# One hybrid attention and scan step on one core: the first projections with features outside, attention with one set of scores

## The chip, the cores and the metric

The kernel runs on one core of one Trainium2 chip. A core has TensorE (PE, matrix products; the loading of stationary operands is shown apart as PEld), VectorE (DVE), ScalarE (ACT), GpSimd (POOL) and SyncE (SP), each with its own row of instructions that it works off in order. PE writes into PSUM, which has eight banks of 512 columns of fp32 in 128 partitions; the other engines read them there. The metric is the device time of one execution in microseconds (us). PE's clock has two levels, 2.4 and 1.2 GHz; "granted clock" is the mean over a stretch in shares of the upper one.

## The reference, cut to what matters

One step of a network with two layers for 128 context tokens and 512 latent tokens of width 1024. The even layer's mixer is attention (8 heads of 64, 2 heads of keys and values, so four query heads share one) beside a gated delta rule (4 heads, both directions); the odd layer's mixer is a state-space scan; each layer also has an MLP. The change touches the first norm, the attention part of the first projection, and attention:

```python
h = _modulate(x, norm_mix_g[layer], sh1, sc1)     # rms norm over features, * (1 + scale) + shift
aq, ak, av, dqkv, dz, dbeta, dalpha = _split(h @ w_in, EVEN_SPLITS)
...
def attend(q_blk):
    s = jnp.einsum('bqhgd,bkhd->bhgqk', q_blk, k, preferred_element_type=F32) * scale
    p = jax.nn.softmax(s, axis=-1).astype(v.dtype)
    return jnp.einsum('bhgqk,bkhd->bqhgd', p, v)
```

Context queries read the 128 context keys; latent queries read 512 latent keys and 256 keys of a cache. Shift and scale come from a vector of conditions by a product with `w_mod`, whose first 2048 columns this stage needs.

## The kernel before, in words

Data is fp32. A large product is split: operands become a high part in fp32r (`hh`, `whi`) and the rest (`hl`, `wlo`), and three fp32r products (`hh·whi`, `hh·wlo`, `hl·whi`) are summed in PSUM. A weight block arrives as `wraw` from HBM, ACT casts it to `whi`, DVE or GpSimd subtracts to `wlo` (`wpart`, L267 to L276; with `share` on, every other subtraction is GpSimd's). Products of attention's scores use fp32r with the high and low parts of queries and keys stacked in the 128 rows of the contraction; weights by values, sums and transposes ("turns", products with the unit matrix `ident`, named `con` in the trace) are in fp32. Which instruction stands where in an engine's row is set by a scheduler that plays the program through with estimated times when it is built; buffers ("pools" with a number of tiles) limit it.

*The start (0 to 88 us).* x, feature-major as `xt` (L727), is loaded in one transfer on ACT's queue. On SP's queue go eight blocks of modulation weights (1.05 MB each, `mod_first`, L497 to L522), and after the first two the weights of attention's first block. `token_r` (L568) works out the norms of one half of the tokens at a time: squares on ACT, sums by PE (`stps`, `stc`), an inverse square root by DVE, and a spreading by PE (`rbps`), copied to `rb`. `modulate` (L599) makes `htmp`, `hh` and `hl` for one feature tile and half after the other. The first projections (`atps`, L750) come in three blocks: 272 columns (gates, keys, values) and twice 256 (queries); for each block and each of five token tiles all eight feature tiles are summed, 24 products, into one of four PSUM tiles.

*Delta projections (88 to 225 us).* `delta_in` (`gps`, L300) projects for the four delta heads, with the preparation of keys (`att_prep`) beside it.

*Attention and delta heads (225 to 508 us).* `attention` is a generator that yields after each step; L775 sets the order in which the program is written, delta head 0, then nine times ten steps of attention, then delta heads 1 to 3; the scheduler mixes their instructions. Attention goes pair by pair of heads (four pairs). `front` makes the scores of a pair with the queries in the rows, only for their maxima (L1273; L1280 and L1285 on DVE). The negated maxima `nm` are turned (L1297) and written into extra rows of `qm`, which face rows of ones in `kst[1]`. `back` makes the scores again with the keys in the rows (L1303, L1304), now with the maximum taken off by those rows, ACT takes the exp (L1330) into a ring `pp` that lies in the raw weights' buffers, and PE multiplies by the values (L1331), where a column of ones gives the sums beside 64 columns of one head: for each pair 12 products of 512 columns. Sums are picked out (L1339), inverted (L1341), spread (L1347) and multiplied (L1350). Front of the next pair runs beside back of this one. Scores, turns and spreads share two PSUM tiles (`psc`), the products with values have one (`pat`).

*Then* the output projection (`by_rows`, `rps` L328) with weights through the same raw buffers, the MLP, the scan layer and its MLP.

## Time and profile before

| | us |
|---|---|
| median of 3 runs | 2151.09 (2150.94 to 2152.92) |
| the profiled execution's own time | 2148.23 |
| its span, first to last instruction | 2146.4 |
| PE busy | 2054.9 |
| DVE busy | 1373.3 |
| ACT busy | 898.4 |
| mean granted clock | 0.976 |

Busy times are those of single engines and overlap. The span is cut into 48 us of start, 40 us of first projections, 137 us of delta projections, 283 us of attention and delta heads up to the first product of the output projection at 512, and 1634 us of the rest. The time of the profiled execution is 2.9 us below the median of the timed runs.

### The profile page before, as it was taken

Reading aid. Unit: us, or ns where it says so; the run is one execution under the profiler, and the core shown is the slowest. Engines: PE = TensorE matmul, PEld = TensorE weight load, DVE = VectorE, ACT = ScalarE, POOL = GpSimd, SP = SyncE. Lnnn points to the kernel's source line nnn. Section 1 sums busy time; section 2 is a strip of 40 time slices with the busy share of each in tenths; the row PEclk is TensorE's granted clock in tenths of the full one; section 3 lists DMA queues with packets and bytes.
Section 4 is the critical chain, followed back from the end, with each engine's and each line's share of the span. In section 5 each row is a group of like instructions: output and inputs, shape, how many; then the busy total and the mean of one; then the engine's idle time right before and its main releaser. Section 6 shows DMA issues by size and latency. Waiting matters only on the chain.

```text
span 2146.4 us, 32954 instructions
## 1 busy us (share of the span) xinstructions
PE 2054.9 (96%) x13339; PEld 1846.3 (86%) x13339; DVE 1373.3 (64%) x2585; ACT 898.4 (42%) x1892; POOL 153.4 (7%) x112
## 2 busy tenths in 40 slices
PE   6999799899899999999899999999999899999998
PEld 4999787787797989898799999999888898989896
DVE  6376776865787767673678886787644734344445
ACT  4345444444342323233258876666531322323131
POOL 1041301300000000000000001111110000000000
PEclk9999799899999999999999999999999999999999
DMA  8261100005255344332224433343341221212121
GB/s 328 91 234 40 39 1 18 18 1 201 80 194 193 138 140 155 138 119 103 89 83 162 132 135 120 120 138 123 107 168 69 89 97 61 79 59 99 59 79 50
DMA packets 56106, 233.32 MB, mean 109 GB/s; under 512 B 6602, under 2 KB 21458, under 8 KB 34194
## 3 DMA queue, kind: packets, MB, share of 16 engines
q1 hardware_dynamic: 45952, 216.63, 28.6%
q10 hardware_dynamic: 10002, 14.58, 1.9%
q8 instruction: 105, 1.72, 0.3%
q14 instruction: 47, 0.39, 0.1%
HBM read 222.76 MB, written 8.43 MB: 108 GB/s over the span
## 4 chain that ended last, share of the span: by engine, by line
PE 89%; DVE 7%; DMA 3%; ACT 1%; issue 1%; DVEq 0%; SPq 0%; ACTq 0%
PE gps L300 41%; PE rps L328 28%; PE atps L750 2%; PE yps L1704 2%; PE avps L1331 2%; DMA wraw<-wall 1%; PE offps L1718 1%; PE dps L1038 1%; PE stps L1735 1%; PE scps L1273 1%; DMA X<-growd 1%; PE dps L1032 1%; PE xkps L1554 1%; PE modps L459 1%; PE scps L1303 1%
## 5 line engine op out<-in xcount | busy, mean ns | idle before, releaser
L300 PE MATMUL gps<-hh,whi 128*128 128x322 f32 (+3 forms) x1552 | 488.4, 316 | 1.4 <-ACT hh L412 1.4
L300 PE MATMUL gps<-hh,wlo 128*128 128x322 f32 (+3 forms) x1552 | 486.4, 314 | 0.0
L300 PE MATMUL gps<-hl,whi 128*128 128x322 f32 (+3 forms) x1552 | 485.3, 313 | 0.0
L300 PEld LDWEIGHTS gps<-hh,whi 128*128 128x128 f32 (+1 forms) x1552 | 292.3, 189 | 7.9 <-issue 4.4
L300 PEld LDWEIGHTS gps<-hl,whi 128*128 128x128 f32 (+1 forms) x1552 | 292.4, 188 | 3.2 <-issue 2.8
L300 PEld LDWEIGHTS gps<-hh,wlo 128*128 128x128 f32 (+1 forms) x1552 | 292.4, 188 | 2.1 <-issue 1.6
L328 PE MATMUL rps<-wlo,hidh 128*128 128x512 f32 x640 | 253.3, 396 | 0.0
L328 PE MATMUL rps<-whi,hidh 128*128 128x512 f32 x640 | 252.3, 396 | 0.0
L328 PE MATMUL rps<-whi,hidl 128*128 128x512 f32 x640 | 250.5, 395 | 0.0
L272 ACT CAST whi<-wraw 128x1024 fp32r<-128x1024 f32 (+2 forms) x132 | 140.0, 1062 | 252.3 <-PE rps L328 176.3
L284 DVE TENSOR_TENSOR wlo<-wraw,whi 128x1024 fp32r<-128x1024 f32 x88 | 107.5, 1224 | 187.4 <-ACT whi L283 187.3
L300 PE MATMUL gps<-yh,whi 128*128 128x320 f32 x1024 | 227.1, 311 | 0.2 <-ACT yh L412 0.2
L275 DVE TENSOR_TENSOR wlo<-wraw,whi 128x1024 fp32r<-128x1024 f32 (+3 forms) x123 | 157.9, 1285 | 101.6 <-ACT whi L272 101.1
L283 ACT CAST whi<-wraw 128x1024 fp32r<-128x1024 f32 x88 | 91.8, 1048 | 266.2 <-PE rps L328 183.3
L300 PEld LDWEIGHTS gps<-yh,whi 128*128 128x128 f32 x1024 | 172.5, 189 | 1.0 <-ACT yh L412 0.7
L300 PE MATMUL gps<-yh,wlo 128*128 128x320 f32 x512 | 158.6, 310 | 0.0
L328 PEld LDWEIGHTS rps<-whi,hidh 128*128 128x128 f32 x640 | 120.3, 188 | 29.4 <-issue 1.2
L328 PEld LDWEIGHTS rps<-wlo,hidh 128*128 128x128 f32 x640 | 120.3, 188 | 28.8 <-issue 0.6
L328 PEld LDWEIGHTS rps<-whi,hidl 128*128 128x128 f32 x640 | 120.3, 188 | 28.6
L485 DVE SCALAR_TENSOR_TENSOR macc<-wraw,condst,macc 128x512 f32<-128x512 f32 x196 | 136.6, 746 | 6.0 <-ACT macc L488 5.9
L650 DVE TENSOR_SCALAR hr<-gps 128x320 f32<-128x320 f32 x128 | 62.6, 489 | 105.8 <-PE gps L300 105.5
L651 ACT ACTIVATE hr<-hr 128x320 f32<-128x320 f32 x128 | 60.1, 470 | 151.8 <-DVE hr L650 150.3
(428 smaller groups left out, 3560.9 us busy)
## 6 DMA issues: line engine op xcount, KB each, us to landing
wraw<-wall SPq DMA_DIRECT2D x158, 1024.0 KB
bc<-afs SPq DMA_DIRECT2D x40, 512.0 KB
Q<-afr SPq DMA_DIRECT2D x64, 128.0 KB
xt<-xt ACTq DMA_DIRECT2D x1, 2560.0 KB
X<-growd SPq DMA_DIRECT2D x8, 320.0 KB
x<-x ACTq DMA_DIRECT2D x1, 2560.0 KB
xd<-x ACTq DMA_DIRECT2D x1, 2560.0 KB
x<-xd SPq DMA_DIRECT2D x1, 2560.0 KB
```

Source lines behind the costliest of these rows:

```text
L272: self.nc.scalar.copy(out=hi, in_=raw[:, :, c:c + m])
L275: eng.tensor_tensor(out=lo, in0=raw[:, :, c:c + m], in1=hi.bitcast(F32), op=ALU.subtract)
L283: self.nc.scalar.copy(out=hi, in_=x)
L284: self.nc.vector.tensor_tensor(out=lo, in0=x, in1=hi.bitcast(F32), op=ALU.subtract)
L300: self.nc.tensor.matmul(ps, ws[k // KT][q // 2][:, k % KT, :], xs[q % 2][k][:, c], start=k == 0 and q == 0, stop=k == n - 1 and q == 2)
L328: nc.tensor.matmul(ps, parts[x][k][:, c], w[y][:, j, :], start=k == 0 and q == 0, stop=k == n - 1 and q == 2)
L485: nc.vector.scalar_tensor_tensor(out=a, in0=x, scalar=w, in1=a, op0=ALU.mult, op1=ALU.add)
L650: nc.vector.tensor_scalar(out=r, in0=ps, scalar1=0.0, scalar2=None, op0=ALU.max)
L651: nc.scalar.activation(out=r, in_=r, func=AF.Square)
L750: nc.tensor.matmul(ps[:, :n], x[k][:, TOFF[t]:TOFF[t] + P], w[:, k, :], start=k == 0 and q == 0, stop=k == KT - 1 and q == 2)
L1331: nc.tensor.matmul(acc, val(c, i), p, start=c == 1, stop=c == 6)
L1704: nc.tensor.matmul(py[q * 64:q * 64 + 64, pr * P:(pr + 1) * P], X[t](1 + d)[:, hh * 64:hh * 64 + 64], D[t][:, d, hh, :], start=d == 0, sto ...
```

## The change

*Start.* x is loaded first, in two halves, on SP's queue, and all further blocks behind it there (`landed`): two modulation blocks, both query blocks of attention, the other six modulation blocks. `token_rows` treats all 640 tokens at once. `mod_first` and `modulate` treat one quarter (two feature tiles) at a time. The query blocks are split into `wqh` and `wql` of 512 columns, and the projection has the features as its outer loop: each two feature tiles add to five PSUM tiles that stay open, 120 products of 512 columns in all (L741 of the kernel after); the 272 columns of gates, keys and values follow as one block (L749). `share` is set only behind that. The pools: open projections 4 to 5 tiles, norms 3 to 2, weights 2 to 1.

*Attention.* Scores are made once, with the queries in the rows: for a tile of 128 queries and one head 768 keys into one PSUM tile of two banks, of which there is one (`psc`; L1242). `softmax` follows: maximum and its scaling on DVE, exp with its sum on ACT (L1251), reciprocal on DVE, and a multiplication by it on ACT (L1254). The finished weights are turned on PE, four 128 × 128 blocks to a bank (`ptps`, L1293), and copied to the ring by DVE and ACT in turn (L1296). Products with values have 64 stationary columns and write rows 0 to 63 for one head and rows 64 to 127 for the other, one after the other (L1302). Turns of queries, turns of weights and products with values share the single tile of `pat`. `qm`, `nm`, the ones beside the values, the sums by product, their spreading and GpSimd's zeroing are gone; the next pair's scores are no longer made beside this pair's products.

```diff
@@ start
-                xload = nc.scalar.dma_start(out=self.xt, in_=io["xt"])
-                rbs = [self.token_r(xp, [self.xt[:, k, :] for k in range(KT)], D, hf) for hf in range(2)]
-                self.mod_first([self.raw, raw0], lambda: watt.append(self.wpart(self.wload(("att", 0), 272, wa), 0, 272, wa)))
-                self.share = True
-                half(0)
-                half(1)
-                for b, (n, c0) in enumerate(blocks):
...
-                    for t in range(NT):
-                        for k in range(KT):
-                                nc.tensor.matmul(ps[:, :n], x[k][:, TOFF[t]:TOFF[t] + P], w[:, k, :],
+                for a in (0, KT // 2):
+                    self.behind = nc.sync.dma_start(out=self.xt[:, a:a + KT // 2], in_=io["xt"][:, a:a + KT // 2])
+                raws = [self.landed(land, ("mod0", 0, kh)) for kh in range(2)]
+                rb = self.token_rows(xp)
...
+                wq = [wa.tile([P, KT, 512], F32R, name=n) for n in ("wqh", "wql")]
+                acc = [self.pg.tile([P, 512], F32, name="atps", tag="g") for _ in range(NT)]
+                for c in range(4):
+                    self.mod_first(c, raws)
+                    if c == 0:
+                        for j in range(2):
+                            x = self.landed(land, ("att", 1 + j)).rearrange("p (k c) -> p k c", c=256)
+                            hi, lo = (w[:, :, j * 256:j * 256 + 256] for w in wq)
+                            nc.scalar.copy(out=hi, in_=x)
+                            nc.vector.tensor_tensor(out=lo, in0=x, in1=hi.bitcast(F32), op=ALU.subtract)
+                    if c < 3:
+                        raws = [self.landed(land, ("mod0", c + 1, kh)) for kh in range(2)]
+                    self.modulate(c, h, xp, rb)
+                    for k in (2 * c, 2 * c + 1):
+                        for t in range(NT):
+                            for q, (x, w) in enumerate(triples(wq)):
+                                nc.tensor.matmul(acc[t], x[k][:, TOFF[t]:TOFF[t] + P], w[:, k, :], start=k == 0 and q == 0, stop=k == KT - 1 and q == 2)
+                wk = self.wpart(self.wload(("att", 0), 272, wa), 0, 272, wa)
...
+                self.turn, self.share = 1, True
@@ attention
-                    for q, x in enumerate((qs, qm)):
-                        nc.tensor.matmul(out, x[:, i, t * P:(t + 1) * P], kst[q][:, kv, k0:k1], start=q == 0, stop=q == 1)
-                        v.tensor_reduce(out=mx[:, 1, t, i:i + 1], in_=sc, axis=AX.X, op=ALU.max)
...
-                    weights(sc, i, c * P, LAT_U)
-                    nc.scalar.activation(out=p, in_=sc, func=AF.Exp, scale=scale)
-                    nc.tensor.matmul(acc, val(c, i), p, start=c == 1, stop=c == 6)
...
+        def softmax(sc, p):
+            v.tensor_reduce(out=mx, in_=sc, axis=AX.X, op=ALU.max)
+            v.tensor_scalar(out=mx, in0=mx, scalar1=-scale, scalar2=None, op0=ALU.mult)
+            for i in range(n):
+                nc.scalar.activation(out=p[:, i], in_=sc[:, i], func=AF.Exp, scale=scale, bias=mx[:, i:i + 1], accum_out=sm[:, i:i + 1])
+            v.reciprocal(out=sm, in_=sm)
+            for i in range(n):
+                nc.scalar.activation(out=p[:, i], in_=p[:, i], func=AF.Copy, scale=sm[:, i:i + 1])
...
+                for t in range(1, NT):
+                    for i in range(2):
+                        sc = psc.tile([P, 2 * 512], F32, name="scps", tag="sc")
+                        scores(sc[:, 0:512], qs, kv, i, t, P, P + 512)
+                        scores(sc[:, 512:768], qs, kv, i, t, P + 512, P + 768)
+                        softmax(sc[:, :768].rearrange("p (o k) -> p o k", o=1), ps[i].rearrange("p (o k) -> p o k", o=1))
+                        yield
+                    for j in range(3):
+                        pt = bank("ptps")
+                        for n in range(4):
+                            nc.tensor.transpose(pt[:, n * P:(n + 1) * P], x, self.ident)
+                        (v.tensor_copy if turn % 2 else nc.scalar.copy)(out=dst, in_=quad(pt))
+                    yield
+                acc = bank("avps")
+                for c in range(6):
+                    for i in range(2):
+                        nc.tensor.matmul(acc[rows[i]], val(1 + c, kv), x, start=c == 0, stop=c == 5)
```

How the rows of the engines change, at the places that the prediction speaks of.

SP's row at the start of the program before: L509 is a modulation block, the L264 row with 2176 columns attention's first block, L561 parameters and constants.

```order
L509 DMA wraw<-wall 128x2048 x2
L264 DMA wraw<-wall 128x2176
L509 DMA wraw<-wall 128x2048 x6
L561 DMA prm<-prm 128x981
L561 DMA con<-cst 128x1024
```

The same place after: L712 is x, L503 the modulation and query blocks in `landed`, L558 parameters and constants.

```order
L712 DMA xt<-xt 128x2560 x2
L503 DMA wraw<-wall 128x2048 x10
L558 DMA prm<-prm 128x981
L558 DMA con<-cst 128x1024
L264 DMA wraw<-wall 128x2176
```

x now leads on SP's queue, and attention's first block went behind all others.

PE's row at the first projections before: L516 are modulation products, L579 and L585 sums of squares, L594 the spreading of norms, L750 projections.

```order
L585 MATMUL stc<-con,st 64x1
L516 MATMUL modps<-wraw,condst 32x128 x32
L594 MATMUL rbps<-con,rr 128x128 x2
L594 MATMUL rbps<-con,rr 128x64
L579 MATMUL stps<-sq,ones_72 32x320 x4
L516 MATMUL modps<-wraw,condst 32x128 x16
L750 MATMUL atps<-whi,hh 128x272
L750 MATMUL atps<-wlo,hh 128x272
L579 MATMUL stps<-sq,ones_72 32x320
```

And after: L513 modulation products, L580 sums, L588 spreading, L741 the projections of queries.

```order
L513 MATMUL modps<-wraw,condst 32x128 x16
L580 MATMUL stc<-con,st 128x1 x5
L588 MATMUL rbps<-con,rr 128x128 x5
L513 MATMUL modps<-wraw,condst 32x128 x16
L741 MATMUL atps<-wqh,hh 128x512
L741 MATMUL atps<-wql,hh 128x512
L513 MATMUL modps<-wraw,condst 32x128 x13
L741 MATMUL atps<-wqh,hh 128x512
L741 MATMUL atps<-wqh,hl 128x512
```

The norms of all tokens now precede the first projection, and modulation products of the next quarter stand between projections of this one.

PE's row in a piece of attention before (`dps` are products of a delta head):

```order
L1331 MATMUL avps<-pp,qkv 128x512
L1273 MATMUL scps<-kst_1586,qs 128x512
L1273 MATMUL scps<-kst_1587,qm_3151 128x512
L1038 MATMUL dps<-Xtc,Xt 128x64 x5
L1066 MATMUL dps<-X,M 64x64 x5
L1273 MATMUL scps<-kst_1586,qs 128x512
L1273 MATMUL scps<-kst_1587,qm_3151 128x512
L1066 MATMUL dps<-X,M 64x64 x5
L1303 MATMUL scps<-qs,kst_1586 128x512
L1304 MATMUL scps<-qm_3150,kst_1587 128x512
L1072 MATMUL dps<-Xt 64x64 x5
```

And after:

```order
L975 MATMUL dps<-dq_755,kT 128x128 x5
L1293 MATMUL ptps<-con,p 128x128 x4
L1037 MATMUL dps<-Xtc,Xt 128x64 x5
L1242 MATMUL scps<-kst_1385,qs 128x512
L1242 MATMUL scps<-kst_1386,qs 128x512
L1242 MATMUL scps<-kst_1385,qs 128x256
L1242 MATMUL scps<-kst_1386,qs 128x256
L1293 MATMUL ptps<-con,p 128x128 x8
L1031 MATMUL dps<-Xc,Xt 128x32 x5
L1242 MATMUL scps<-kst_1385,qs 128x512
```

Between the scores of one unit and the next there now stand turned weights and delta products; the products with values come together at the end of a pair.

## Rows read from the trace of the kernel before

**Rows 1.** The page: busy time by engine; shares of the chain by engine

```profile
PE 2054.9 (96%) x13339; PEld 1846.3 (86%) x13339; DVE 1373.3 (64%) x2585; ACT 898.4 (42%) x1892; POOL 153.4 (7%) x112
...
PE 89%; DVE 7%; DMA 3%; ACT 1%; issue 1%; DVEq 0%; SPq 0%; ACTq 0%
```

**Rows 2.** Five stretches: length, busy time of PE, PEld, DVE, ACT, POOL, granted clock, DMA share, GB/s

```profile
0.00:48.00 48.00, 26.95 (x368) 20.91 (x368) 27.99 (x93) 19.43 (x43) 4.74 (x5) 0.96 0.90 366
48.00:88.00 40.00, 40.00 (x322) 40.00 (x323) 14.69 (x34) 10.85 (x23) 3.60 (x2) 0.96 0.22 83
88.00:225.00 137.00, 135.78 (x1221) 130.76 (x1221) 96.53 (x195) 65.27 (x180) 35.59 (x28) 1.00 0.34 119
225.00:260.00 35.00, 24.01 (x126) 19.37 (x125) 27.83 (x66) 15.11 (x48) 15.79 (x13) 0.80 0.23 59
260.00:508.00 248.00, 234.67 (x1591) 196.92 (x1590) 169.75 (x454) 113.02 (x286) 31.89 (x24) 0.93 0.08 26
```

**Rows 3.** Timeline of PE, first projections: start, length, instruction, count [idle before <- releaser]

```profile
29.24 0.60 PE L750 MATMUL atps<-whi,hh 128*128 128x272 f32 x1
...
47.89 0.39 PE L750 MATMUL atps<-whi,hl 128*128 128x272 f32 x1 [3.55 <-DVE hl L624]
```

**Rows 4.** Chain that ended last, pieces: start, length, what; two stretches

```profile
61.98 25.38 PE atps L750 x216
...
643.78 14.00 PE rps L328 x60
```

**Rows 5.** DVE's groups by form, 0 to 90: busy, mean ns | idle before

```profile
L624 DVE SCALAR_TENSOR_TENSOR hl<-htmp,mod,hh 128x320 fp32r<-128x320 f32 x8 | 4.2, 541 | 0.0
L275 DVE TENSOR_TENSOR wlo<-wraw,whi 128x2048 fp32r<-128x2048 f32 x1 | 2.3, 2291 | 1.4 <-ACT whi L272 1.4
```

**Rows 6.** PE's groups by form, 225 to 512

```profile
L1339 PE MATMUL scps<-con,au 128*128 128x1 f32 x80 | 11.0, 262 | 1.0 <-DVE au L1334 1.0
L1263 PE MATMUL scps<-con,pp 128*128 128x128 f32 x40 | 7.5, 313 | 0.0
```

**Rows 7.** Timeline of PE at four places, for intervals between starts

```profile
225.64 0.93 PE L1263 MATMUL scps<-con,pp 128*128 128x128 f32 x7
226.41 0.71 PE L937 MATMUL dps<-con,dk 128*128 128x128 f32 x5
...
482.81 0.39 PE L1095 MATMUL dps<-s,Xt 128*128 128x128 f32 x2
483.03 1.02 PE L1331 MATMUL avps<-pp,qkv 128*128 128x512 f32 x2
...
484.35 1.02 PE L1331 MATMUL avps<-pp,vc 128*128 128x512 f32 x2
...
503.78 1.31 PE L1347 MATMUL scps<-con,ar 128*64 128x128 f32 x20
505.02 0.49 PE L1106 MATMUL ops<-s,qd 128*128 128x128 f32 x2
...
578.98 1.94 PE L409 MATMUL hps<-con,hrow 128*128 128x128 f32 x8 [6.93 <-DVE hrow L403]
```

**Rows 8.** PE's waits, 225 to 512: waited for, us in total, times, longest

```profile
PE scps L1273 <- DVE mx L1280: 3.9, 4, 1.7
...
PE scps L1273 <- DVE mx L1285: 1.3, 4, 0.5
...
PE scps L1303 <- DVE mx L1280: 0.3, 1, 0.3
```

**Rows 9.** DVE's and ACT's groups by form, 225 to 512

```profile
L1285 DVE TENSOR_REDUCE mx<-scps 128x1 f32<-128x512 f32 x32 | 21.6, 684 | 6.9 <-PE scps L1273 6.6
...
L1330 ACT ACTIVATE pp<-scps 128x512 f32<-128x512 f32 x48 | 27.7, 594 | 44.2 <-PE scps L1304 44.0
...
L636 ACT CAST op<-ota 128x640 fp32r<-128x640 f32 x4 | 2.9, 726 | 8.4 <-DVE ota L1350 8.3
```

**Rows 10.** Timeline of PE at the first product of the output projection

```profile
512.14 2.07 PE L328 MATMUL rps<-whi,op 128*128 128x512 f32 x4 [4.09 <-ACT whi L283]
```

More of the change, by code (lines that the diff above doesn't have):

```diff
@@ L1227, in attention @@
[L1227 removed]
+        nc, v = self.nc, self.nc.vector
+        kst, vc = keys
         scale = 64.0 ** -0.5
[L1230 to L1238 removed]
@@ L1353, in attention @@
[L1353 to L1365 removed]
+            return qs
```

324 lines of the change are left out of this document (120 added, 204 removed).

## The prediction

> **What bounds the kernel now.** I read the engine shares first [rows 1]: TensorE (PE) is busy for 96% of the span and holds 89% of the chain that ended last. So a step counts if it takes products off PE or fills a time in which PE stands. Next come five stretches [rows 2]. In the first, 0 to 48 us, PE works 27 of 48 us while the DMA engines are 90% busy at 366 GB/s: the start is bound by loading. From 48 to 225 PE is full (40.0 of 40, 135.8 of 137). From 225 to 508, attention with the delta heads, it is busy for 24.0 + 234.7 of 283 us; the other two big engines are far from full there (VectorE (DVE) 27.8 + 169.8, ScalarE (ACT) 15.1 + 113.0). The granted clock is 0.80 and 0.93 there, so 35 × 0.20 + 248 × 0.07 = 24 us of it go to the lower of PE's two clock levels, another 24 are idle, and some 235 us are products at full clock. Behind 508 the same work stands before and after, and I give it 0 ± 3. The change thus has three places: the start up to the last first projection, the stage of attention, and the hand-over to the output projection. The delta projections between (88 to 225) are PE-bound with the same products: 0 ± 2.
>
> **Part 1, the start.** What it removes: before, x (2.6 MB on ACT's queue) and the modulation blocks share the bandwidth, the first projection starts at 29.24 us, PE still waits 3.55 us for DVE's modulate at 47.89 [rows 3], and the last projection ends at 61.98 + 25.38 = 87.4 [rows 4]. PE has 360 products of some 0.12 us to do (25.38 us for 216) [rows 4], 43 us in all, and most of them stand behind 48: 322 records of all kinds lie between 48 and 88 [rows 2]. Now x goes first, then two modulation blocks, then both query blocks, all on one queue: 2.6 + 4 × 1.05 = 6.8 MB. At 366 GB/s [rows 2] that is 18.6 us, from some 2 us on: the last query block is there at 20 to 21. Then ACT casts it and DVE subtracts (2.29 us for 2048 columns [rows 5], and I give the cast as much). Both subtractions stand ahead of the copy of the norms in DVE's row, so that the first feature's modulate (0.54 us a piece for 320 columns [rows 5], two pieces for each group of tokens) ends near 27.5. From there PE has no other bound: 120 products of 512 columns at 14.00/60 = 0.233 [rows 4] are 28.0 us, 120 of 272 columns at 0.125 are 15.0, three modulation blocks cost 3, and I put 2 for modulation products that stand in PE's row before their block has landed or its features are ready. Covered: two features take DVE about 2 × 2.4 us, PE 30 × 0.233 = 7.0; a pair of blocks of 2.1 MB lands every 5.7 us. If DVE fell behind PE by 1 us for each of the other seven features, 7 us would come back. Sum: 27.5 + 28 + 15 + 3 + 2 = 75.5, say 76, against 87.4: **−11 us**. The ends: −16 (first product at 24, no waits) and −4 (first product at 32, waits of 5). GpSimd splits no weights there any more; it did little (4.7 us in 48 [rows 2]), and DVE's part is in the sum.
>
> **Part 2, attention on PE.** Prices from intervals between starts. A 512-column product of weights by values: from 483.03 to 484.35 PE does one such product and two 512-column score products [rows 7], so 1.32 − 2 × 0.233 = 0.855 us. A 128-column product in this precision leaves two records: two of them from 482.81 to 483.03 [rows 7], 0.22 for both records. A turn of 128 × 128 leaves one (40 for the 40 turns of the queries [rows 6]): seven from 225.64 to 226.41 [rows 7], 0.11 each. Ten 64-row products in alternating halves take from 503.78 to 505.02 [rows 7], 0.124 each instead of 0.22, a factor of 0.56.
> For each of the four pairs of heads go: the second scores, 24 × 0.233 + 0.3 for the context = 5.9; the turns of the maxima, 5 full products = 1.1; the weights by values, 12 × 0.855 + 2 × 0.22 = 10.7; the sums, 20 records (80 in four pairs [rows 6]) at 0.11 = 2.2; the spreading of the reciprocals, 1.2. Together 21.1. For each pair come: 50 turns, 50 × 0.11 = 5.5; twelve products side by side, 12 × 0.855 × 0.56 = 5.7; the context's two, 0.25. Together 11.5. Saved: 9.6 a pair, **−38 us**. The scores that stay cost the same (two 512 and two 256 products for a tile and head).
>
> **Part 3, the waits of attention.** Seven entries of PE's waits name attention's old steps, from 3.9 us for the scores behind the maxima down to 0.3 [rows 8]: 3.9 + 1.8 + 1.3 + 1.0 + 0.7 + 0.6 + 0.3 = 9.6 us, and they go. New: a unit (one tile of one head, 32 in all and four small ones) writes its scores into the only score buffer, and this is free again after DVE's maximum over 768 columns (0.684 for 512 [rows 9], so about 0.96), the scaling (0.2) and ACT's exp (0.594 for 512 [rows 9], about 0.85): some 2.3 us behind the unit's last product with the hops. In ACT's row the normalising of 768 columns stands behind it (0.726 for 640 [rows 9], so 0.85), on which the turns wait; every bank of turned weights then waits for a copy by DVE or ACT in turn (for 512 columns some 0.6 to 0.7, as the maximum and the exp of 512) before the single turn bank is free. What PE has in its row between two units, at the prices above, is mostly 2 to 3.7 us of turns and delta products; in seven places it is 0.4 to 1.8. These seven alone give some 7 us. The rest hangs on how late DVE and ACT come. DVE loses 50 us in the stage (maxima 33, products with the reciprocals 8, copies and small ones 9) and gains 65 (maxima 31 + 2, scaling and reciprocals 13, copies 19), so about 15: 198 + 15 = 213 us. ACT gains some 40: 168. If the stage shrinks from 283 to some 255, DVE is busy for 83% of it; before it was 68% from 260 on, and 80% in the 35 us ahead, where PE was busy for only 24 [rows 2]. So a unit will often find DVE at delta work. I take 0.7 us a unit, the 0.65 that PE waited for a maximum in eight entries (3.9 + 1.3 us [rows 8]) where nothing covered it, and the seven thin places on top: 36 × 0.7 = 25; minus 9.6 that is **+15 us**. Bounds: only the thin places (7, so −3) and 1.2 a unit, DVE late by one delta operation of some 0.5 each time (43, so +34).
>
> **Part 4, the hand-over.** Before, PE stands for 4.09 us until 512.14, since ACT splits the first weights of the output projection only then [rows 10]. These weights' buffers are those that attention uses as its ring. Now the last weights-by-values products are PE's last work of the stage and read that ring, so a load that needs it starts later; before, sums and spreading came behind. Only the later blocks hang on the ring, and x is asked for earlier: **+2 us**, from 0 to +8 (a block of 1.05 MB at 366 GB/s, and a split).
>
> **Sum.** −11 − 38 + 15 + 2 = −32 us against the profiled execution of 2148.2, which lies 3 us under the median of the runs shown; I carry the difference over to the median: 2151.1 − 32 = 2119.
>
> **Rivals.**
> *DVE's maxima in front of the only score buffer become the bound (slower).* Place: the 32 units. Start, products and hand-over give −11 − 38 + 2 = −47, and the old waits −9.6; so the kernel gets slower once the new waits pass 57 us, 1.6 a unit, which makes a stage of about 292 us and a DVE that is busy for 73% of it. If DVE stays at the 70% that it has there now (198 of 283), the stage takes 213 / 0.70 = 304 us, 21 more than now: 2151 − 11 + 21 + 2 = 2163. For it: DVE is ahead of PE in work there (213 against 203), and each unit passes through it twice, once for the maximum and once for turned weights. Against it: the 80% of the window from 225, and the order, which puts delta products between most units. The Trainium skill, Perfetto Trace Analysis, Optimizing Tensor Performance (Matmuls), speaks against this change: independent groups of products should rotate through different PSUM banks, so that evacuating one overlaps the next. By that rule one score buffer makes every unit wait, which is this rival; the waits on maxima in the rows, short as they are even with two buffers, agree with it in kind. Chance 0.19.
> *The turns cost double.* If PE runs the 200 turns at the lower clock level, as eight did behind an idle time of 6.93 us (1.94 us, 0.24 each instead of 0.11 [rows 7]), they cost 200 × 0.11 = 22 us more: 2141. Against it: seven in a row at 0.11 in the middle of other work, and turns here stand between products everywhere. The Trainium skill, TensorE: Matmul & The Clock Gate, Part 4 (PE-mode transpose), says that transposes do not count as work that raises the clock; by that rule this is how it goes, and the seven turns at 225.64 speak against it. Chance 0.05.
> *The two heads' products do not overlap (the change doesn't do what it says).* Then twelve products cost 10.3, not 5.7: +18 us, 2137. The row at 503.78 speaks against it. Chance 0.05.
> *The start gives nothing away.* If x, the splits and the modulate on DVE put the first projection at 36 and PE then waits feature by feature, only −1 is left: 2129. For it: DVE's modulate held PE back for 3.55 us before, too [rows 3]. Chance 0.09.
>
> **How the numbers follow.** My forecast has 0.62, from 2097 (both gains full, only the thin places) to 2152 (all the bad ends together); of it 0.60 is faster, 0.02 within the bound. The start's rival gives 0.08 faster and 0.01 the same, the overlap's 0.05 faster, the turns' 0.03 faster and 0.02 the same, the slower one 0.16 slower and 0.03 the same. Faster 0.76, same 0.08, slower 0.16, with 0.2% (4.3 us) about what a measurement of this kernel can tell from no change. The range 2100 to 2155 leaves out the slower rival and little else.
>
> **What would show it.** In the new profile the first 512-column projection starts at 27 to 28 us and the last 272-column one ends at 74 to 77. From the first turn of queries to the output projection the stage is some 20 us shorter; two side-by-side products stand 0.96 apart, turns 0.11. PE's waits name the maxima, the exp and the copies of turned weights, 17 to 35 us in all; DVE is busy for over 78% of the stage. The idle before the output projection is 4 to 12 us. I am wrong if PE's waits on these pass 57 us, if the clock in the stage falls below 0.85, or if the projections end behind 83.

## The result and the profile after

The changed kernel takes 2176.66 us (median of 4, 2176.23 to 2177.03) against 2151.53 (2150.94 to 2152.92): a ratio of 1.0121, 95% interval 1.0108 to 1.0134. It is **25 us slower**, where 32 us less were forecast, and above the range given (2100 to 2155).

The page after, with the busy shares and the chain that answer to [rows 1]:

```profile
span 2174.8 us, 32558 instructions
...
PE 2055.7 (95%) x13103; PEld 1843.6 (85%) x13103; DVE 1370.9 (63%) x2595; ACT 933.4 (43%) x1940; POOL 144.4 (7%) x105
...
PE 84%; DVE 6%; ACT 2%; DMA 1%; issue 1%; POOL 0%; DVEq 0%; ACTq 0%; SPq 0%
```

PE's busy time is what it was (2055.7 against 2054.9), although some 38 us of products were taken out: PE did less work and did it slower. To see where, both traces are cut at the same places: end of the first projections, end of the last delta projection, first product of the output projection, end. First before (columns as in [rows 2]: length, PE, PEld, DVE, ACT, POOL, granted clock, DMA share, GB/s):

```profile
87.40:224.73 137.33, 136.11 (x1224) 131.11 (x1224) 97.13 (x195) 65.63 (x181) 35.59 (x28) 1.00 0.34 119
224.73:512.14 287.41, 259.00 (x1717) 216.55 (x1716) 200.21 (x529) 131.46 (x344) 47.68 (x36) 0.91 0.11 35
```

And after:

```profile
82.80:234.47 151.67, 141.82 (x1233) 136.35 (x1234) 97.85 (x211) 65.30 (x176) 32.95 (x23) 0.97 0.29 107
234.47:537.78 303.31, 250.40 (x1610) 214.11 (x1608) 213.31 (x590) 166.93 (x419) 48.76 (x36) 0.80 0.11 32
537.78:2174.00 1636.22, 1595.61 (x9714) 1440.36 (x9714) 1029.95 (x1723) 673.19 (x1303) 59.14 (x41) 0.99 0.33 114
```

The projections end 4.6 us earlier (82.8 against 87.4), the delta projections take 14.3 us more, attention 15.9 more, and the rest 2.8: 28 us of span. Of a stretch I use four numbers below. **Idle** is its length less PE's busy time. **Loss** is its length times one less the granted clock, as the expectations below count it; it includes idle time at the lower level, and the clock has two digits, so ±1.5 us. **Busy loss** is the part of it in which PE is busy: half of PE's busy time at the lower level, by the clock's own records in the trace. **Work** is busy time less busy loss, what PE would need at the upper level. Idle, busy loss and work add up to the length. For attention they were 28, 21 and 238 us before, and 53, 51 and 200 after (the loss 26 and 61). PE's work fell by 38 us, as forecast; idle time rose by 25 and the busy loss by 30, so the stage got 16 us longer.

*The start.* PE's timeline after, at the end of the projections (start, length, instruction, count, idle before and its releaser):

```profile
82.49 0.29 PE L749 MATMUL atps<-whi,hl 128*128 128x272 f32 x1
88.44 1.87 PE L903 MATMUL gps<-gg,con 128*128 128x20 f32 x8 [5.67 <-issue]
90.94 0.40 PE L910 MATMUL gps<-con,gc 128*40 128x128 f32 x1 [0.62 <-ACT ek L906]
90.99 0.62 PE L300 MATMUL gps<-hh,whi 128*128 128x322 f32 x1
...
92.48 0.47 PE L300 MATMUL gps<-hh,wlo 128*128 128x322 f32 x1
...
97.12 0.31 PE L300 MATMUL gps<-hh,wlo 128*128 128x322 f32 x1
```

DVE's timeline after, the last instruction of the gates' chain:

```profile
88.14 0.20 DVE L898 SCALAR_TENSOR_TENSOR gg<-gg,gea 128x40 f32<-128x40 f32 x1
```

And before:

```profile
67.80 0.20 DVE L899 SCALAR_TENSOR_TENSOR gg<-gg,gea 128x40 f32<-128x40 f32 x1
```

L903 is a small product of the gates (decay sums of the delta heads). It needs a softplus that DVE works out in some 15 small instructions from the gates' columns, and these columns are now in the last block of projections. It stands in PE's row ahead of the first delta projection, so PE is idle for 5.67 us until the chain's end at 88.34 (the row names no releaser; the times do), and the clock falls: a delta projection's records are 0.47 us long until 97, 0.31 behind. Before, the gates' block was the first, and the chain ran beside the query blocks, which ended 19 us after it.

*Attention.* PE's waits from 234 to 538 (us in total, times, longest), which answer to [rows 8]:

```profile
PE ptps L1293 <- ACT p L1254: 6.7, 6, 2.6
PE scps L1242 <- ACT p L1251: 5.5, 6, 3.2
PE kvps L869 <- ACT qs L1237: 4.9, 1, 4.9
PE dps L1145 <- DVE M L1144: 4.6, 4, 2.0
PE dps L1037 <- DVE amx L1249: 4.2, 3, 3.1
PE dps L1031 <- DVE Xc L971: 4.2, 1, 4.2
...
PE rps L328 <- ACT whi L283: 3.0, 1, 3.0
PE dps L1031 <- DVE amx L1249: 2.6, 1, 2.6
```

The score buffer itself (L1242 behind the exp) costs 5.5 us, the normalising (L1254) 6.7; but delta products, too, now wait for DVE, where the scaling of a maximum (`amx`) is the last to end in 6.8 us of their waits. The larger part is the clock. Four stretches of the stage after (columns as above):

```profile
278.00:284.50 6.50, 3.42 (x22) 2.67 (x22) 6.44 (x15) 2.59 (x5) 2.64 (x2) 1.00 0.00 0
284.50:300.00 15.50, 14.88 (x67) 14.50 (x67) 9.06 (x22) 6.47 (x11) 0.00 (x0) 0.50 0.01 2
300.00:315.20 15.20, 15.20 (x73) 14.99 (x73) 7.54 (x16) 4.08 (x11) 0.00 (x0) 0.50 0.00 0
315.20:325.00 9.80, 9.80 (x76) 5.73 (x74) 4.67 (x20) 2.08 (x5) 0.00 (x0) 0.99 0.01 2
```

PE is idle for half of 6.5 us while DVE is full; the clock falls to its lower level, and stays there for 30.7 us **in which PE is never short of work** (30.1 us busy). From 417.7 on there is another of 27.3 us. What PE did in the first (groups by form: busy, mean ns of one):

```profile
L1031 PE MATMUL dps<-Xc,Xt 128*128 128x32 f32 x50 | 11.0, 393 | 2.6 <-DVE amx L1249 2.6
L1037 PE MATMUL dps<-Xtc,Xt 128*128 128x64 f32 x41 | 9.1, 409 | 0.0
L1293 PE MATMUL ptps<-con,p 128*128 128x128 f32 x20 | 5.4, 426 | 0.0
L1024 PE MATMUL dps<-X,M 128*128 128x128 f32 x10 | 2.5, 437 | 0.0
L1242 PE MATMUL scps<-kst,qs 128*128 128x512 f32 x4 | 2.4, 701 | 0.0
L1024 PE MATMUL dps<-Xt 128*128 128x128 f32 x10 | 2.3, 421 | 0.0
L1242 PE MATMUL scps<-kst,qs 128*128 128x256 f32 x4 | 1.3, 415 | 0.0
```

Mostly products of 32 and 64 columns of a delta head and turns, with some delta products of 128 columns and the scores of two units. At 315 the clock rose, 1 us before the first products with values of 512 columns at 316.4, so it wasn't these that raised it there. In the stage before, products with values stand in some 29 places from 263 to 501; after, only at the ends of the four pairs (from 316, 388, 471 and 525).

### The profile page after: what moved, and what is told of

Same layout as the page of the kernel before. It is cut to its first block, busy times and chain, and to the rows that moved or that the text cites. A ratio compares the mean times of both kernels' runs of the same rounds, so it can differ in the third digit from the quotient of the medians.

```text
span 2174.8 us, 32558 instructions
## 1 busy us (share of the span) xinstructions
PE 2055.7 (95%) x13103; PEld 1843.6 (85%) x13103; DVE 1370.9 (63%) x2595; ACT 933.4 (43%) x1940; POOL 144.4 (7%) x105
## 4 chain that ended last, share of the span: by engine, by line
PE 84%; DVE 6%; ACT 2%; DMA 1%; issue 1%; POOL 0%; DVEq 0%; ACTq 0%; SPq 0%
PE gps L300 41%; PE rps L328 28%; PE yps L1647 2%; PE offps L1661 1%; PE dps L1037 1%; PE dps L1031 1%; PE scps L1242 1%; PE stps L1678 1%; DMA X<-growd 1%; PE ptps L1293 1%; PE avps L1302 1%; PE xkps L1497 1%; PE modps L459 1%; PE hps L409 0%; PE dps L1024 0%
## 5 line engine op out<-in xcount | busy, mean ns | idle before, releaser
L272 ACT CAST whi<-wraw 128x1024 fp32r<-128x1024 f32 (+1 forms) x130 | 136.5, 1052 | 260.8 <-PE rps L328 176.6
L275 DVE TENSOR_TENSOR wlo<-wraw,whi 128x1024 fp32r<-128x1024 f32 (+1 forms) x122 | 153.8, 1262 | 104.8 <-ACT whi L272 104.6
```

Of the source, the lines that this page charges most:

```text
L272: self.nc.scalar.copy(out=hi, in_=raw[:, :, c:c + m])
L275: eng.tensor_tensor(out=lo, in0=raw[:, :, c:c + m], in1=hi.bitcast(F32), op=ALU.subtract)
```

## The experiments

Each is measured against the kernel before on the same chip. Nearly every edit also moves the scheduler's order in attention: in run 11, whose attention is the changed one, 1163 of the changed kernel's 1608 records of PE in the stage keep their order; in run 5, 915. Several kernels spread by 10 us and more from one execution to the next, so differences of under some 5 us between them are not read. The stage's numbers come from the one profiled execution of a kernel, which can lie off the median: in runs 1, 3, 6, 8 and 12 it is 4 to 8 us above.

| kernel | median us | ratio (95%) | delta projections end | attention | idle | loss | busy loss | work |
|---|---|---|---|---|---|---|---|---|
| before | 2151.5 | 1 | 224.7 | 287.4 | 28 | 26 | 21 | 238 |
| changed | 2176.7 | 1.0121 (1.0108 to 1.0134) | 234.5 | 303.3 | 53 | 61 | 51 | 200 |
| 1 start only | 2169.2 | 1.0090 (1.0067 to 1.0114) | 235.4 | 298.6 | 30 | 39 | 31 | 238 |
| 2 attention only | 2150.7 | 1.0002 (0.9987 to 1.0018) | 225.8 | 286.3 | 49 | 46 | 38 | 200 |
| 3 turns as products | 2158.6 | 1.0039 (1.0024 to 1.0054) | 231.5 | 292.6 | 39 | 35 | 32 | 221 |
| 4 gates first, old attention | 2141.3 | 0.9961 (0.9946 to 0.9976) | 224.2 | 281.7 | 24 | 23 | 20 | 237 |
| 5 no maxima | 2136.3 | 0.9931 (0.9908 to 0.9953) | 234.5 | 267.6 | 34 | 37 | 34 | 200 |
| 6 diagonal | 2168.4 | 1.0065 (1.0044 to 1.0087) | 234.5 | 298.8 | 38 | 45 | 40 | 221 |
| 7 gates first, diagonal | 2150.6 | 1.0003 (0.9989 to 1.0017) | 223.5 | 291.3 | 39 | 35 | 30 | 222 |
| 8 and tile by tile | 2139.2 | 0.9940 (0.9918 to 0.9963) | 223.6 | 284.2 | 34 | 26 | 23 | 227 |
| 9 gates first, tile by tile | 2138.7 | 0.9932 (0.9910 to 0.9953) | 223.1 | 281.4 | 45 | 39 | 33 | 204 |
| 10 lighter DVE | 2132.8 | 0.9913 (0.9887 to 0.9940) | 223.7 | 276.1 | 32 | 17 | 13 | 232 |
| 11 gates first | 2150.2 | 0.9993 (0.9979 to 1.0007) | 223.5 | 289.0 | 52 | 43 | 37 | 201 |
| 12 head 1 earlier | 2128.9 | 0.9890 (0.9873 to 0.9907) | 223.4 | 278.0 | 34 | 19 | 18 | 226 |
| 13 wide fp32 added | 2173.3 | 1.0102 (1.0085 to 1.0119) | 234.5 | 302.6 | 51 | 30 | 23 | 228 |
| 14 wide fp32r added | 2163.8 | 1.0056 (1.0031 to 1.0080) | 231.1 | 294.2 | 50 | 41 | 36 | 208 |

The work column can be tested: kernels with the same products in attention agree (before, 1 and 4; changed, 2, 5 and 11), and the 32 products added in run 13 raise it by 28 us, where 27 is their price.

**1. The changed start with attention as before**, and **2. the start as before with the changed attention** (each takes one half of the diff):

> The changed start and first projections, with attention as before. Theory (the start itself gives nothing back: the projections end 4.8 us earlier, but then PE stands for the gates' chain and the clock falls behind it): 10 us later than before at the end of the delta projections, so about 2160 us (2156 to 2164). Rival (the start gains its 5 us, and the loss behind it comes from the new attention's order): about 2146 us.

> The start as before, with the changed attention. Theory (attention alone costs 16 us by idle time and the lower clock level): 2165 to 2171 us, and the stage's granted clock at 0.80 to 0.83. Rival (attention gains what was forecast where the start doesn't shift it): about 2130 us.

The rows of attention in runs 1, 2 and 11:

```profile
235.36:533.99 298.63, 268.43 (x1717) 223.56 (x1715) 197.44 (x536) 132.25 (x344) 47.82 (x36) 0.87 0.12 37
225.80:512.12 286.32, 237.15 (x1610) 203.28 (x1608) 209.01 (x590) 168.44 (x419) 47.88 (x36) 0.84 0.11 34
223.47:512.44 288.97, 237.45 (x1610) 202.77 (x1609) 208.63 (x590) 167.36 (x419) 47.46 (x36) 0.85 0.11 33
```

The start alone costs 18 us, more than the theory's 5 to 13. In the profiled execution (2174.8) some 11 are there at the end of the delta projections (235.4), as the theory had it; 11 more are in an attention whose work is the old one (238) and whose loss is larger (39 against 26), and some 5 behind it. Attention alone costs nothing and gives nothing, where both theory (16 slower) and rival (20 faster) missed: 39 us of work went, 21 came back as idle time and 17 as busy loss. The two halves add up to some 18 us where the whole change costs 25; run 1's spread (2162.5 to 2174.8) leaves open whether they hinder each other.

**3. Turns of weights as ordinary products** with the unit matrix:

```diff
-                            nc.tensor.transpose(pt[:, n * P:(n + 1) * P], x, self.ident)
+                            nc.tensor.matmul(pt[:, n * P:(n + 1) * P], x, self.ident, start=True, stop=True)
```

> The changed kernel with the turns of weights as ordinary products with the unit matrix instead of transposes; nothing is left out. At full clock they cost 200 x 0.11 = 22 us more. Theory A (idle time is what takes the clock down): the clock in the attention stage stays at or below 0.83, and the time is 2185 to 2200 us. Theory B (transposes are what keeps the clock low, ordinary products would raise it): the granted clock of the stage goes to 0.88 or more, and the time is 2160 to 2178 us.

The stage's row (compare that of the changed kernel above):

```profile
231.45:524.08 292.63, 253.33 (x1810) 223.56 (x1809) 206.98 (x590) 167.79 (x419) 45.91 (x36) 0.88 0.11 33
```

21 us more work (22 were expected), and 18 us less time, just below theory B's range: the clock is at 0.88, as theory B said. But idle time fell by 14 us as well, and the order moved, so by this run alone the mode of the turns, the idle time and the order can't be told apart. In the profiled executions 3 us of the gain stand ahead of attention (231.5 against 234.5), where the edit changes no product.

**4. The gates' block first**, with attention as before. Features outside and five open sums for the 272 columns, then the 512 columns of queries by token tiles:

```diff
-                acc = [self.pg.tile([P, 512], F32, name="atps", tag="g") for _ in range(NT)]
+                acc = [self.pg.tile([P, 512], F32, name="atps", tag="g")[:, :272] for _ in range(NT)]
...
-                            for q, (x, w) in enumerate(triples(wq)):
-                                nc.tensor.matmul(acc[t], ...)
+                            for q, (x, w) in enumerate(triples(wk)):
+                                nc.tensor.matmul(acc[t], ...)
...
-                for t in range(NT):
-                    ps = self.pg.tile([P, 512], F32, name="atps", tag="g")[:, :272]
+                for t in range(NT):
+                    ps = self.pg.tile([P, 512], F32, name="atps", tag="g")
+                    for k in range(KT):
+                        for q, (x, w) in enumerate(triples(wq)):
```

> Attention as before; the changed start, but the block with gates, keys and values has the features outside and comes first, and the 512 columns of queries follow token tile by token tile, so that the gates' chain on DVE and ACT runs beside 28 us of products. Theory (the gates' chain behind the last block is what cost the start its gain): the wait of 5.7 us goes and the projections end at 75 to 78 us, so 10 to 18 us less than the run with the start alone: 2142 to 2150 us. Rival (the start is bound by loads and DVE whatever the order): within 4 us of the run with the start alone.

28 us less than run 1, and 10 us less than before. Its stretches:

```profile
0.00:80.70 80.70, 67.61 (x551) 52.42 (x551) 36.32 (x94) 28.35 (x46) 6.01 (x6) 0.98 0.66 259
80.70:224.22 143.52, 138.41 (x1234) 132.58 (x1233) 97.09 (x193) 66.27 (x181) 41.60 (x28) 1.00 0.32 114
224.22:505.93 281.71, 257.43 (x1718) 215.49 (x1716) 195.71 (x520) 128.59 (x331) 47.53 (x36) 0.92 0.10 31
```

The 5.7 us of idle time at L903 are gone and the clock is at 1.00 behind the projections. In the profiled executions 11 us lie there (224.2 against 235.4) and 17 in attention, where the loss went from 39 to 23 at the same work (the 5 behind it come with run 1's slow execution). Yet the start itself is hardly better than the old one (224.2 against 224.7): the projections end at 80.7, not at the 75 to 78 expected, and the stretch behind them is 6 us longer than before (143.5 against 137.3). Of these, 4 are idle time, mostly waits of PE for DVE's `vt` and `dv` (3.5 us, before 0.7).

**5. The maxima left out:** DVE's maximum and its scaling go, the exp takes a hundredth of the score unshifted.

```diff
-            v.tensor_reduce(out=mx, in_=sc, axis=AX.X, op=ALU.max)
-            v.tensor_scalar(out=mx, in0=mx, scalar1=-scale, scalar2=None, op0=ALU.mult)
...
-                nc.scalar.activation(out=p[:, i], in_=sc[:, i], func=AF.Exp, scale=scale, bias=mx[:, i:i + 1], accum_out=sm[:, i:i + 1])
+                nc.scalar.activation(out=p[:, i], in_=sc[:, i], func=AF.Exp, scale=scale * 0.01, accum_out=sm[:, i:i + 1])
```

> The changed kernel without the maxima: the exp isn't shifted (it takes a hundredth of the score), so DVE's maximum and its scaling are left out for all 36 units; everything else stands. Theory A (the chain through DVE before the only score buffer is what costs idle time and, by it, the clock): idle time of PE in the attention stage falls by 12 us or more, the granted clock rises to 0.87 or more, 2145 to 2160 us. Theory B (the turns as transposes hold the clock down whatever the waits are): the clock stays at or below 0.83 and the time at 2163 to 2175 us.

```profile
234.54:502.14 267.60, 233.47 (x1606) 200.96 (x1604) 171.81 (x500) 164.45 (x411) 45.77 (x36) 0.86 0.13 41
```

40 us less than the changed kernel, all in the stage (36): DVE has 42 us less to do, PE's idle time falls by 19, the busy loss by 17. The turns are transposes here as there. So the maxima are behind 19 of the 25 us by which idle time rose, and more than half of the rise in busy loss goes with them. This is theory A, with the time 9 us below its range and the clock (0.86) just short of its 0.87. The edit takes away a link of the chain and 42 us of DVE's work at once, and it moves the order of the row: which of these does it is not told apart.

**6. The diagonal of reciprocals** in place of the unit matrix (on run 3), **7.** the same behind the start of run 4:

```diff
-                nc.scalar.activation(out=p[:, i], in_=p[:, i], func=AF.Copy, scale=sm[:, i:i + 1])
+                nc.scalar.activation(out=dg[i], in_=self.ident, func=AF.Copy, scale=sm[:, i:i + 1])
```

> The run with the turns as ordinary products, and the unit matrix replaced by a diagonal of the reciprocals, so that ACT scales 128 columns for each unit instead of 768 (0.3 to 0.4 us instead of 0.85) and the turns wait for less. Theory (the normalising on ACT costs the 5.9 us of waits that PE showed for it, and some of the waits for copies behind it in ACT's row): 2146 to 2154 us, against 2158.6 with full normalising. Rival (the next link, exp or copies, takes the wait over): 2156 to 2161 us.

> The same attention (turns as products with the diagonal) behind the start with the gates' block first. Theory (the two losses add up): the start's order gave 28 us against the start alone, so some 20 to 28 us below the run with the diagonal alone, 2120 to 2134 us. Rival (the stage of attention gives the gain back): 2141 us or more, no better than the old attention behind this start.

Run 6 is a miss: no gain over run 3, rather a loss of 10 with a spread of 17 us between its executions (2155 to 2172). The waits on the scaling fell only from 5.9 to 3.8 us, those on ACT's copies went from 5.5 to 6.2. Run 7 misses its theory, too (2120 to 2134): it is 18 us below run 6, 11 of them at the end of the delta projections, so the start's part adds up, but no more than to the time of before, as the rival had it.

**8. Products with values tile by tile** (on run 7), **9.** the same with transposes and the full normalising:

```diff
+                    acc = bank("avps")
+                    for c in range(6):
+                        for i in range(2):
+                            nc.tensor.matmul(acc[rows[i], :P], val(1 + c, kv), pb[:, 4 * i + c if c < 4 else 4 + 2 * i + c], start=c == 0, stop=c == 5)
+                    nc.scalar.copy(out=o[:, LAT_U][:, cols], in_=acc[:, :P])
```

> As the last, but weights by values are multiplied tile by tile (12 products of 128 columns side by side behind each tile's turns) instead of 12 of 512 columns at the end of a pair. Theory (products spread over the pair cover waits and shorten the hand-over at the end): 3 to 8 us below the last. Rival (the single bank that turns and products share now also waits for a copy for every tile): the same, or up to 6 us above.

> The gates' block first and products tile by tile, but turns as transposes and the full normalising on ACT, as in the changed kernel; only the start and the place of the products with values differ from it. Theory A (the granted clock follows PE's idle time, whatever the turns are): in the attention stage the time lost to the lower level stands to the idle time as 0.75 to 1.3, as in all runs so far, and idle time is 38 to 48 us: 2140 to 2155 us. Theory B (transposes hold the clock down by themselves): the loss is more than 1.4 times the idle time, the clock below 0.84, 2155 to 2170 us.

Spreading these products over the stage takes 11 us off (8 against 7, more than the 3 to 8 expected; 9 against 11). The loss falls from 35 to 26 in run 8, although no product with values is wider than 128 columns any more; from 43 to 39 in run 9 is within what one program shows (runs 10 and 12 below). Run 9 has less work than run 8 (204 against 227) and more idle time and loss (45 and 39 against 34 and 26), and takes the same time. Theory A's ratio holds in it: loss over idle is 0.88 (and the time 1 us below its range), so 200 transposes in the stage do not by themselves force it past 1.4, though the longest stretch at the lower level of all kernels (34.1 us) stands in this run.

**10. Less on DVE:** queries scaled by −1/8 where they are split, a minimum as the shift, two of three copies of turned weights on ACT. **12.** Delta head 1 written after four parts of attention.

```diff
-            v.tensor_reduce(out=mx, in_=sc, axis=AX.X, op=ALU.max)
-            v.tensor_scalar(out=mx, in0=mx, scalar1=-scale, scalar2=None, op0=ALU.mult)
+            v.tensor_reduce(out=mx, in_=sc, axis=AX.X, op=ALU.min)
...
-                        (v.tensor_copy if turn % 2 else nc.scalar.copy)(out=dst, in_=quad(pt))
+                        (v.tensor_copy if turn % 3 == 0 else nc.scalar.copy)(out=dst, in_=quad(pt))
...
-            for ch in "0abcdefghi123":
+            for ch in "0abcd1efghi23":
```

> The run with products tile by tile and the diagonal, with less work on DVE: queries are scaled by -1/8 where they are split, so that a minimum over the scores is the shift itself and the 36 scalings of the maximum go, and two of three banks of turned weights are copied by ACT instead of one of two; nothing is left out. Theory (DVE's lateness in front of the score buffer is what is left): 11 us less on DVE, 6 to 12 us below the 2139.2 of that run, 2127 to 2133 us. Rival (ACT, now later with its copies, takes the place): 2136 to 2142 us.

> The fastest kernel so far (2132.8 us) with delta head 1 written after four parts of attention instead of nine, so that two delta heads can fill PE's idle time beside the later units; the same work. Theory (idle time is what costs both itself and the clock, and more delta products beside attention fill it): idle time below 28 us and 2120 to 2130 us. Rival (DVE, which both need, only gets later): 2133 to 2145 us.

Run 10 is the fastest kernel of this study, 19 us below before and at the upper end of its theory's range. It didn't gain its 6 us over run 8 as the theory had it: DVE's busy time in the stage is 201.8 us against 203.4, not 11 less, and idle time 32 against 34; what fell is the loss (17 against 26). Run 12 is the same program: the scheduler sets the instructions as it did in run 10, and all rows of PE (13591 records), DVE, ACT and GpSimd are the same, with the same operands. So its theory was not tested, and its 4 us, idle time of 34 and loss of 19 show how far one program differs from itself (2127.8 to 2137.3 over both).

**11. The changed kernel with the gates' block first:**

> The changed kernel with one thing else: the block with gates, keys and values has the features outside and comes first, the queries' block follows by token tiles; attention is the changed one, untouched. Theory (the start's order costs what it cost with the old attention, and the lower clock in attention is idle time's): 11 us at the end of the delta projections, so 2160 to 2168 us; the products tile by tile are then worth the rest down to 2138.7. Rival (how the start ends also sets what attention loses): 2140 to 2155 us, and the products tile by tile are worth little.

26 us less, by one change of order in the first 80 us; 11 of them at the end of the delta projections. The other 14 are again in attention, at equal work (201 against 200), equal idle time (52 against 53) and less loss (43 against 61). The rival was right on the time, and on what the start does to attention; that the products tile by tile are then worth little was not (11 us, run 9). With this start the changed attention costs nothing against before (2150.2), so the order of the start's two blocks is what made the change slower. This left open why the clock stayed down without idle time, which the last two runs ask.

**13. and 14. One unused wide product for each unit**, in fp32 (the first line) and in fp32r (the second), into the score buffer that the scores then write over:

```diff
+                        nc.tensor.matmul(sc[:, 0:512], self.ident, qkv[:, t, 272:784], start=True, stop=True)
+                        nc.tensor.matmul(sc[:, 0:512], qs[:, i, t * P:(t + 1) * P], kst[0][:, kv, P:P + 512], start=True, stop=True)
                         scores(sc[:, 0:512], qs, kv, i, t, P, P + 512)
```

> The changed kernel with one product more for each of the 32 units: 512 columns in fp32 (unit matrix by queries) into the score buffer ahead of the scores, which write over it; the result is unused. Its price at full clock is 32 x 0.855 = 27 us. Theory (in the stage of attention the clock stays low because, without the wide products with values between them, PE's row holds only narrow delta products, turns and scores): the two stretches of 27 and 31 us at the lower level go, the loss to it falls from 61 us by 25 or more, and the whole is 2160 to 2182 us in spite of the added work. Rival (only idle time sets the clock): the loss falls by no more than the idle time does, 2188 to 2204 us.

> The same with a 512-column product in fp32r (queries by keys, once more), 32 x 0.233 = 7.5 us at full clock. Theory (any wide product raises the clock): the loss to the lower level falls by 15 us or more, 2155 to 2172 us. Rival (only idle time, or only the long fp32 products matter): the loss within 8 us of the changed kernel's 61, 2177 to 2186 us.

The stage of run 13, beside that of the changed kernel above:

```profile
234.50:537.09 302.59, 251.18 (x1674) 199.43 (x1673) 206.95 (x590) 168.63 (x419) 46.36 (x36) 0.90 0.10 32
```

And of run 14:

```profile
231.13:525.35 294.22, 244.60 (x1643) 206.97 (x1641) 205.27 (x590) 169.11 (x419) 48.17 (x36) 0.86 0.11 33
```

In run 13 PE has 28 us **more** work, the same idle time (51 against 53), and the stage takes the same time: the loss went from 61 to 30 (the busy loss from 51 to 23), and no stretch at the lower level is longer than 13.7 us. In run 14 the work rises by 8, the loss falls by 20 (the busy loss by 14), and the kernel is 13 us faster, though 3 of these stand ahead of attention (231.1 against 234.5), one long stretch (27.3 us) is left and the spread is wide (2152 to 2173). Idle time alone can't do this: at 50 to 53 us of it the busy loss was 51, 37, 36 and 23 (changed kernel, runs 11, 14, 13). But the order of the row moved, too (1237 and 1286 of the 1608 records keep theirs in 13 and 14), and in run 11 order alone took 14 us of busy loss away. So run 14 need not show more than that, and of run 13's 28 us the added products' own share is not told apart.

## Why the prediction was wrong, point by point

- **Part 1, up to the end of the projections**: −4.6 us, near the upper bound of −4 that was given. The first product of 512 columns was forecast at 27.5 and came at 28.07, 272 columns took the 15 us of the sum (67.55 to 82.6). Between them stood 39.5 us, not 33: three modulation blocks cost some 6 us instead of 3, and some of the products ran at the lower level (0.43 us from start to start at 60 us, instead of 0.233). The same start ended at 82.8 to 84.1 us in five kernels (the changed one, runs 1, 5, 6 and 13).
- **Part 1, behind the projections**: this is the first step that failed. "The delta projections between are PE-bound with the same products: 0 ± 2" measured +14.3. The sum ended with the last projection and did not ask what needs the block that was moved last. The gates' chain on DVE and ACT had been covered by query products; moved behind them it stood alone, in front of all delta projections in PE's row. Runs 1, 4 and 11 show it: with the gates' block first, 11 us come back at this point with either attention, 2 to 3 of them up to the end of the projections and 8 to 9 behind. The other 6 of the 14 stay with the gates first (run 4); what is seen of them are waits for DVE, and why these grew is open.
- **Part 2, PE's work**: right. −38 forecast, −38 measured as work. Twelve products side by side took 5.30 us (0.44 each; 0.48 forecast), a turn 0.12 (0.11).

The rows for these, PE's timeline after:

```profile
28.07 0.73 PE L741 MATMUL atps<-wqh,hh 128*128 128x512 f32 x1
...
67.55 0.30 PE L749 MATMUL atps<-whi,hh 128*128 128x272 f32 x1
...
252.64 0.66 PE L1293 MATMUL ptps<-con,p 128*128 128x128 f32 x4 [1.48 <-ACT p L1254]
253.13 1.06 PE L975 MATMUL dps<-dq,kT 128*128 128x128 f32 x8
...
316.42 3.65 PE L1302 MATMUL avps<-pp,qkv 128*64 128x512 f32 x16
319.91 1.89 PE L1302 MATMUL avps<-ppr,vc 128*64 128x512 f32 x8
321.72 0.44 PE L1065 MATMUL dps<-X,M 64*64 64x64 f32 x4
```

- **Part 3, the waits**: idle time rose by 25 us, where +15 was forecast with an end of +34: in range. The sum itself left out a term: the 7 us of the seven thin places are named as coming on top, but 36 × 0.7 = 25 doesn't hold them; with them it is +22. The mechanism was right in kind (run 5: without the maxima 19 us of it go). What was missing is that delta products wait for DVE's maxima as well, 6.8 us in the rows above for L1037 and L1031.
- **The clock in attention** is the second step that failed, and the largest: +30 us of busy loss (the loss went from 26 to 61) for which the sum had no term. The rows to doubt by were there: [rows 2] showed 0.80 and 0.93 in this stage, and the first section even worked out 24 us of loss from them, but the sum then treated this as a constant, although one of the three signs of being wrong was a clock below 0.85 in the stage. It was 0.80. Part of the rise goes with idle time (run 5: 19 us less idle time, 17 less busy loss). Part does not: run 11 changed it by 14 us, with the same work and idle time in another order. What in a row's order does this stays open. That the change itself raised it by taking 512-column products out fits run 13, but isn't shown: order moved there as well, and run 8 has less loss than 7 with narrower products, spread out.
- **Part 4**: PE stands 3.0 us before the output projection; +2 was forecast, −1 measured. The rest of the program is 2.8 us longer, within the ± 3 given.
- **The rivals.** The slower one (DVE's maxima before the only score buffer, 0.19) named the right place and a time of 2163. The stage that it gave, 304 us with DVE busy for 70%, is what was measured (303.3 and 213.3 us of DVE), but by luck: it wanted 57 us and more of waits at the buffer, and only 5.5 us of PE's waits are for it, while busy loss alone makes the stage 30 us longer. (It put PE's work at 203 us; its own rows give 235 − 38 = 197, and 200 was measured.) The Trainium skill's rule on rotating groups through PSUM banks (Perfetto Trace Analysis, Optimizing Tensor Performance) thus points the right way, with a small part of the time behind it; a second score buffer wasn't tried, since all eight banks are in use. The rival on turns at the lower level (0.05) was priced at +22 us, with transposes alone in mind. The row held against it, seven turns at 0.11, came directly behind wide delta projections and said nothing about turns in the middle of attention. The Trainium skill (TensorE: Matmul & The Clock Gate, Part 4) says that transposes do not count as work that raises the clock. The runs agree in direction: the loss is smaller where turns are ordinary products (35 against 61 in run 3, 26 against 39 in run 8 beside run 9). Idle time is smaller there too, so the mode's own share stays open. "The start gives nothing away" left −1 of the start's −11 by a late first product (36 us); that product came at 28.07, and the loss stood behind the projections.

## What to carry to other kernels

Before a block is moved to the end of a stage, list everything that hangs on its result and price that chain as bare: the gates' 16 columns cost more than the 512 columns won. Where the granted clock of a stage is below 1, it is a term of the sum with a range of its own: here the same products at the same idle time were granted 0.80 or 0.85 by their order alone (changed kernel, run 11), and work that was taken out came back as slower work and as waits. A stage's busy time can stay nearly the same (250 us against 259) while its work falls by a sixth; busy time times granted clock shows it.

## What the runs showed that was not expected

- Adding 32 unused products of 512 columns in fp32 (28 us of work) left the time about as it was (2173.3 against 2176.7), and adding 32 in fp32r (8 us) came out 13 us faster.
- The clock can stay at its lower level for 30.7 us while PE is busy for 30.1 of them, with delta products of 32 to 128 columns, turns and the scores of two units in its row.
- The order of two blocks in the first 80 us moved the stage from 235 to 538 us by 14 us, at equal work and idle time (run 11): through the scheduler's order and the clock, which this study does not separate.
- Another order of writing (run 12) can give the same program: compare the rows before reading the times.
